# A hybrid streaming layer on one core: the input turned by VectorE, the first weights split as one piece, squares and parameters taken at other places

## The chip, the cores and the metric

One Trainium2 core runs one launch of the kernel. The metric is the device time in microseconds (us), the median over runs. Engines: PE (TensorE) multiplies, PEld is its weight load, DVE is VectorE, ACT is ScalarE, POOL is GpSimd, SP is SyncE, which here only issues DMAs.

## The reference

One layer of a streaming trunk, for 256 prompt tokens and 32 sample tokens (288 columns in all), model width 2048, in fp32:

```python
xn = rmsnorm(x, p['norm_mix_pre'])
proj = xn @ p['w_in']          # columns u 1024 | z 2048 | xBC 2560 | dt 32
u, z, xbc, dt_raw = proj[..., :o1], proj[..., o1:o2], proj[..., o2:o3], proj[..., o3:]
y_pool, new_pool = pool_mixer(u, hist_pool, pos, ...)         # trailing means, 4 groups
y_ssd, new_sconv, new_h = ssd_mixer(z, xbc, dt_raw, ...)      # conv, silu, exact chunked scan, gated norm
mix = jnp.concatenate([y_pool, y_ssd], axis=-1) @ p['w_out']
x = x + rmsnorm(mix, p['norm_mix_post'])
up = rmsnorm(x, p['norm_ffn_pre']) @ p['w_up']                # 2 x 5632 columns
...
f = (jax.nn.silu(gate) * val) @ p['w_down']
x = x + rmsnorm(f, p['norm_ffn_post'])
```

The new states (pooling rows, convolution rows, scan state, FFN rows) are returned too. The change touches the first lines only: the norm of x and the first columns of `proj`.

## The kernel before

Activations are kept feature-major: a K tile holds 128 features on the partitions and the 288 tokens as columns. Weights are the stationary operand, 128 x 128 at a time. Products of fp32 precision are made of three matmuls of rounded parts (`mm3`, L162 to L165): high weight by high activation, high weight by low activation, low weight by high activation. `split_w` (L134) makes the weight's parts: a ScalarE copy for `whi` (L146) and a VectorE subtraction for `wlo` (L147), 1024 columns at a time. `split_from` (L110) makes the activation's, `xn`: L120 on ScalarE with the norm's gain as scale, L121 on VectorE. `project` (L167) runs a list of column groups over the K tiles, with up to five PSUM accumulators (`acc`); three more banks (`aux`) serve everything else. The root mean square is not applied to `xn`, but to the results, as `rstd`, when they leave the accumulators.

The projections of w_in come in this order: a first group of 544 columns (B and C, 512, and dt, 32), then the convolved channels xs in groups of 256 columns, z and u among them; the scan's pieces of work lie between the later ones. The order on each engine is found by a scheduler that simulates the program; `high_priority` moves work ahead in it, `issue_after` and `keep_in_program_order` tie an instruction to another or to the order of the text. A buffer pool with four `raw` buffers holds weights as they land, so SP's issue of a load waits for the buffer's last reader.

The first group runs in K pieces of 2, 2, 4, 4 and 4 tiles. For each piece SP loads the tokens of x (rows on partitions, L294, L295) and the three pieces of weights (256, 256 and 32 columns). `input_tiles` (L292) turns each K tile by three PE transposes (L299 to L301) into an `aux` bank; ScalarE and VectorE read `xn` from there, and VectorE copies the tile to `xT` (L304). ScalarE's queue stores `xT` to DRAM (L306); it is loaded again much later for the residual. The dt columns are split by `split_narrow` (L151), two parts side by side, so that two matmuls of 64 columns (L185, L186) serve them.

The squares for the norm are three ScalarE instructions of 2048 columns with an accumulated sum (L348, L349), then square root, reciprocal, and PE matmuls that spread the result over the partitions (L355), then a copy to `rstd`. `parameters()` (L309), called ahead of the last K piece, turns rows of small parameters by PE (`columns`, L278) with VectorE copies behind.

The DMAs of SP's and of ScalarE's queue share eight completion semaphores in turn: a load waits until the one eight before it has landed.

Of the kernel before, what the change touches and what calls it, by code (L numbers as in the profile page):

```python
# [8 lines left out]
F32 = mybir.dt.float32  # L9
# [7 lines left out]
P = 128  # L17
TC = {"schedule_with_timeline_sim": True}
D_MODEL = 2048
NP_ = 256  # L20
# [20 lines left out]
Z_RATE = (1, 0, 1, 1, 0, 1, 1, 0)  # L41
TAIL = NT - P


@with_exitstack
def body(
# [78 lines left out]

    ahead = [0]

    def fetch_w(view, kb, nk, c0, nc_):
# [21 lines left out]

    def split_narrow(raw, kb, nk, nc_, after):  # L151

        both = xin.tile([P, nk, 2, nc_], F32R, tag="both", bufs=2, name="both")
        with ExitStack() as order:
            order.enter_context(tc.high_priority(offset=ahead[0]))
            for ins in after:
                order.enter_context(tc.issue_after(ins.ins))
            act.activation(both[:, :, 0, :], raw, AF.Copy)
            dve.tensor_tensor(both[:, :, 1, :], raw, both[:, :, 0, :].bitcast(F32), op=ALU.subtract)
        return [(kb + k, both[:, k, :, :].rearrange("p r c -> p (r c)")) for k in range(nk)]  # L160

    def mm3(out, wh, wl, a, start, stop):  # L162
        pe.matmul(out, wh, a[:, 0, :], start=start, stop=False)  # L163
        pe.matmul(out, wh, a[:, 1, :], start=False, stop=False)  # L164
        pe.matmul(out, wl, a[:, 0, :], start=False, stop=stop)  # L165

    def project(view, groups, acts, ksplit, before=None, done=None, spare=(), hold=(), behind=None):  # L167

# [6 lines left out]
        for i, (kb, n) in enumerate(ksplit):  # L175
# [5 lines left out]
            for raw, (c0, w) in zip(raws, groups):  # L181
                if w < P:
                    for k, both in split_narrow(raw, kb, n, w, after or ()):
                        o = accs[m0][: 2 * w, :]
                        pe.matmul(o, both, acts[k][:, 0, :], start=k == k_first, stop=False)  # L185
                        pe.matmul(o, both, acts[k][:, 1, :], start=False, stop=k == k_last)  # L186
                    continue
                parts = split_w(raw, kb, n, w, ((after or ()) if m0 else ()) + (hold if i else ()))
# [23 lines left out]


    ident = const.tile([P, P], F32, name="ident")
    make_identity(nc, ident)
    ones = const.tile([P, P], F32, name="ones")
    pool.memset(ones, 1.0)
    tri = const.tile([P, P], F32, name="tri")
# [5 lines left out]
    warm = const.tile([P, 1], F32, name="warm")  # L224
    tc.keep_in_program_order(act.activation(warm, eps_t, AF.Copy))
    rec = const.tile([P, 16], F32, name="rec")
# [20 lines left out]

    start = ExitStack()
    xin = start.enter_context(tc.tile_pool(name="xin", bufs=1))

    g0_in = xin.tile([KD, P], F32, name="g0_in")
    act.dma_start(out=g0_in, in_=rows(norm_mix_pre))
    pb_in = xin.tile([108, P], F32, name="pb_in")
# [3 lines left out]
    pool.dma_start(out=pb_in[92:108, :], in_=rows(norm_ffn_post))  # L257
    xt = xin.tile([P, 2, D_MODEL], F32, name="xt")
    xs_ = xin.tile([NS, D_MODEL], F32, name="xs_")
    xpv = x_prompt.rearrange("o (b p) d -> p (o b) d", p=P)  # L260
    pa_in = xin.tile([124, P], F32, name="pa_in")
# [15 lines left out]

    def columns(src, n, name):  # L278
        o = const.tile([P, n], F32, name=name)
        p_ = aux([P, n], "pt")  # L280
        pe.transpose(p_, src, ident[:n, :n])
        dve.tensor_copy(o, p_)
        return o

    g_mix_pre = columns(g0_in, KD, "g0")


    xn = []
    xT = xin.tile([P, KD, NT], F32, name="xT")
    xT_d = dram.tile([P, KD, NT], F32, name="xT_d")  # L290

    def input_tiles(kb, n):  # L292
        c = slice(kb * P, (kb + n) * P)
        sp.dma_start(out=xt[:, :, c], in_=xpv[:, :, c])  # L294
        sp.dma_start(out=xs_[:, c], in_=x_sample[0][:, c])  # L295
        for t in range(kb, kb + n):
            p_ = aux([P, NT], "pt")
            c = slice(t * P, (t + 1) * P)
            pe.transpose(p_[:, 0:P], xt[:, 0, c], ident)  # L299
# [4 lines left out]
            dve.tensor_copy(xT[:, t, :], p_)  # L304
            xn.append(a)
        act.dma_start(out=xT_d[:, kb : kb + n, :], in_=xT[:, kb : kb + n, :])  # L306
        return last

    def parameters():  # L309
        pb = columns(pb_in, 108, "pb")  # L310
        g_mix_post = pb[:, 60:76]
        g_ffn_pre = pb[:, 76:92]
        g_ffn_post = pb[:, 92:108]
        pa = columns(pa_in, 124, "pa")
        pah = const.tile([P, 100], F32, name="pah")
        act.activation(pah, pa[:, 0:100], AF.Copy, scale=0.5)
        p_scale = pa[:, 100:108]
        g_ssd = const.tile([P, NX], F32, name="g_ssd")
        act.activation(g_ssd, pa[:, 108:124], AF.Copy, scale=0.5)
        pc = columns(pc_in, 120, "pc")  # L320
        pf = const.tile([P, 6, NF * 2], F32, name="pf")
        for i in range(0, 6, 3):
            p_ = aux([P, 3, NF * 2], "ptf")
            for j in range(3):
                pe.transpose(p_[:, j, :], pf_in[:, i + j, :], ident[: NF * 2, : NF * 2])
            dve.tensor_copy(pf[:, i : i + 3, :], p_)
        return pb, pah, g_mix_post, g_ffn_pre, g_ffn_post, pa, p_scale, g_ssd, pc, pf

    prm = []

    def first_in(kb, n):
        if kb == 12:
            prm.extend(parameters())
        return input_tiles(kb, n)

    win = w_in.rearrange("o (k p) c -> p (o k) c", p=P)
    O_Z, O_X = D_POOL, D_POOL + D_SSD
    O_B, O_C, O_DT = O_X + D_SSD, O_X + D_SSD + 256, O_X + CONV
    first = project(
        win, [(O_B, 256), (O_C, 256), (O_DT, HEADS)], xn, [(0, 2), (2, 2), (4, 4), (8, 4), (12, 4)], first_in  # L340
    )

    ahead[0] = 200
    ssum = xin.tile([P, 3], F32, name="ssum")
    pool.memset(ssum, 1.0)
    junk = xin.tile([P, D_MODEL], F32, name="junk")
    for b in range(2):
        act.activation(junk, xt[:, b, :], AF.Square, accum_out=ssum[:, b : b + 1])  # L348
    act.activation(junk[:NS, :], xs_, AF.Square, accum_out=ssum[:NS, 2:3])  # L349
    rs = xin.tile([P, 3], F32, name="rs")  # L350
    act.activation(rs, ssum, AF.Sqrt, bias=eps_t, scale=1.0 / D_MODEL)
    dve.reciprocal(rs, rs)
    p_ = aux([P, NT], "prs")
    for b, (o, n) in enumerate(BLK):
        pe.matmul(  # L355
            p_[:, o : o + n], rs[:n, b : b + 1].broadcast_to([n, P]), ident[:n, :n], start=True, stop=True
        )
    rstd = const.tile([P, NT], F32, tag="spread", bufs=3, name="rstd")
    dve.tensor_copy(rstd, p_)

    pb, pah, g_mix_post, g_ffn_pre, g_ffn_post, pa, p_scale, g_ssd, pc, pf = prm
    start.close()
# [45 lines left out]

    xs_ps = [project(win, [(O_X, 256)], xn, K16)]
    xs_in = {}  # L410
# [465 lines left out]
    for grp in ((0, 1), (2,), (3,), (4,), (5,), (6,), (7,)):  # L876
# [9 lines left out]
        if grp[0] == 0:  # L886
            sp.dma_start(out=xT, in_=xT_d)
            state_out(sc_stage.rearrange("p s r t -> p s (r t)"), 60, (rows4(new_sconv_p), rows4(new_sconv_s)), op_)
# [146 lines left out]
    fd = dram.tile([NT, D_MODEL], F32, name="fd")  # L1035
    pin = tc.keep_in_program_order

# [184 lines left out]
```

## Time and profile before

| | us |
|---|---|
| median of 3 runs | 1354.11 (1353.88 to 1354.45) |
| the profiled execution, its own time | 1354.27 |
| its span | 1352.6 |
| PE busy | 1340.1 (99%) |
| VectorE busy | 886.6 (66%) |
| ScalarE busy | 669.5 (50%) |
| GpSimd busy | 233.2 (17%) |

The profile is one execution. A group of instructions is given as line, engine, operation, output and inputs with shapes, count, then busy time and mean duration in ns, then the engine's idle time before them with what ended it. A wait row gives what an engine waited for: total, times, longest. A matmul's duration covers its passage through the array; successive ones overlap, so the pitch (start to start) is what counts.

### The profile page before, as it was taken

The numbers are of one execution on the slowest core, as the hardware profiler recorded it, in microseconds if no ns is written. First come the engines' busy times: TensorE is split into PE (matmuls) and PEld (weight loads), VectorE is DVE, ScalarE is ACT, GpSimd is POOL, SyncE is SP. The second block draws the span as 40 slices with busy tenths as digits, with TensorE's granted clock in tenths as the row PEclk, the third lists the DMA queues.
The fourth block names the chain that finished last, engine by engine and source line by source line (L and its number), as shares of the span: only waits on it lengthen the run. The fifth ranks groups of instructions, "written<-read, shape, count | busy, mean of one in ns | idle before, by whom it ended". The sixth has DMA issues, their size and how long they took to land.

```text
span 1352.6 us, 25723 instructions
## 1 busy us (share of the span) xinstructions
PE 1340.1 (99%) x10199; PEld 1327.7 (98%) x10199; DVE 886.6 (66%) x1519; ACT 669.5 (50%) x1003; POOL 233.2 (17%) x394
## 2 busy tenths in 40 slices
PE   8999999999999999999999999999999999999997
PEld 7999999999999999999999999999999999999997
DVE  6898988779644479977676644335666666664454
ACT  6557767446534455645444433334444444454443
POOL 3132112222223320211121100001111111101110
PEclk9999999999999999999999999999999999999999
DMA  8869985464756546876545545554554554576663
GB/s 269 250 192 280 257 249 167 154 221 151 243 179 201 159 132 191 239 196 182 183 156 163 173 144 169 172 179 156 175 168 156 175 169 156 170 232 181 191 182 94
DMA packets 300135, 252.13 MB, mean 186 GB/s; under 512 B 75728, under 2 KB 293050, under 8 KB 299886
## 3 DMA queue, kind: packets, MB, share of 16 engines
q1 hardware_dynamic: 296942, 243.46, 59.0%
q0 software_dynamic: 2320, 4.65, 1.2%
q10 hardware_dynamic: 752, 2.37, 0.5%
q8 instruction: 80, 1.31, 0.4%
q14 instruction: 41, 0.34, 0.1%
HBM read 236.13 MB, written 14.31 MB: 185 GB/s over the span
## 4 chain that ended last, share of the span: by engine, by line
PE 99%; DVE 0%; DMA 0%; ACT 0%; issue 0%; DVEq 0%
PE acc L163 31%; PE acc L165 31%; PE acc L164 31%; PE pst L852 1%; PE py L562 1%; PE acc L1128 1%; PE acc_x L164 0%; PE acc_x L163 0%; PE acc_x L165 0%; PE py L564 0%; DMA xt<-in_x_prompt 0%; PE pt L299 0%; PE acc L1129 0%; PE pt L301 0%; DVE wlo L147 0%; PE acc L186 0%
## 5 line engine op out<-in xcount | busy, mean ns | idle before, releaser
L147 DVE TENSOR_TENSOR wlo<-raw,whi 128x1024 fp32r<-128x1024 f32 (+1 forms) x416 | 493.3, 1188 | 347.9 <-ACT whi L146 346.6
L146 ACT ACTIVATE whi<-raw 128x1024 fp32r<-128x1024 f32 (+1 forms) x416 | 426.6, 1028 | 498.0 <-PE acc L164 421.0
L163 PE MATMUL acc<-hn,whi 128*128 128x288 f32 x1376 | 404.1, 295 | 0.0
L164 PE MATMUL acc<-hn,whi 128*128 128x288 f32 x1376 | 403.6, 294 | 0.3 <-DVE hn L911 0.3
L165 PE MATMUL acc<-hn,wlo 128*128 128x288 f32 x1376 | 403.1, 294 | 0.0
L164 PEld LDWEIGHTS acc<-hn,whi 128*128 128x128 f32 x1376 | 259.7, 189 | 0.7 <-DVE hn L911 0.7
L165 PEld LDWEIGHTS acc<-hn,wlo 128*128 128x128 f32 x1376 | 259.6, 189 | 0.0
L163 PEld LDWEIGHTS acc<-hn,whi 128*128 128x128 f32 x1376 | 257.2, 187 | 0.1
L163 PE MATMUL acc<-xn,whi 128*128 128x288 f32 x704 | 209.3, 299 | 0.0
L164 PE MATMUL acc<-xn,whi 128*128 128x288 f32 x704 | 208.0, 296 | 0.0
L165 PE MATMUL acc<-xn,wlo 128*128 128x288 f32 x704 | 207.2, 296 | 0.0
L163 PE MATMUL acc<-fa,whi 128*128 128x288 f32 x682 | 201.9, 296 | 0.0
L164 PE MATMUL acc<-fa,whi 128*128 128x288 f32 x682 | 201.9, 296 | 0.0
L165 PE MATMUL acc<-fa,wlo 128*128 128x288 f32 x682 | 201.5, 295 | 0.0
L164 PEld LDWEIGHTS acc<-xn,whi 128*128 128x128 f32 x704 | 133.6, 190 | 0.3
L165 PEld LDWEIGHTS acc<-xn,wlo 128*128 128x128 f32 x704 | 132.9, 189 | 0.3
L163 PEld LDWEIGHTS acc<-xn,whi 128*128 128x128 f32 x704 | 132.4, 189 | 0.5
L164 PEld LDWEIGHTS acc<-fa,whi 128*128 128x128 f32 x682 | 128.6, 188 | 0.0
L163 PEld LDWEIGHTS acc<-fa,whi 128*128 128x128 f32 x682 | 128.1, 188 | 0.0
L165 PEld LDWEIGHTS acc<-fa,wlo 128*128 128x128 f32 x682 | 127.9, 188 | 0.0
L945 POOL COPY fc_stage<-ebuf 128x4 f32<-128x4 f32 x88 | 27.8, 316 | 503.6 <-DVE ebuf L944 460.2
L951 DVE SCALAR_TENSOR_TENSOR fc<-ebuf,pf,fc 128x290 f32<-128x290 f32 x176 | 90.4, 517 | 3.1 <-ACT fc L949 0.5
(341 smaller groups left out, 1660.7 us busy)
## 6 DMA issues: line engine op xcount, KB each, us to landing
raw<-in_w_up SPq DMA_DIRECT2D x80, 1024.0 KB, 5.2
raw<-in_w_in SPq DMA_DIRECT2D x40, 1024.0 KB, 5.7
raw<-in_w_down SPq DMA_DIRECT2D x32, 1024.0 KB, 5.3
raw<-in_w_out SPq DMA_DIRECT2D x24, 1024.0 KB, 5.6
raw<-in_w_down SPq DMA_DIRECT2D x16, 768.0 KB, 5.0
raw<-in_w_up SPq DMA_DIRECT2D x14, 512.0 KB, 4.1
gb<-g_d SPq DMA_DIRECT2D x8, 832.0 KB, 5.4
raw<-in_w_in SPq DMA_DIRECT2D x6, 512.0 KB, 6.0
```

Of the source, the lines that this page charges most:

```text
L146: act.activation(hi, raw[:, k : k + n, :], AF.Copy)
L147: dve.tensor_tensor(lo, raw[:, k : k + n, :], hi.bitcast(F32), op=ALU.subtract)
L163: pe.matmul(out, wh, a[:, 0, :], start=start, stop=False)
L164: pe.matmul(out, wh, a[:, 1, :], start=False, stop=False)
L165: pe.matmul(out, wl, a[:, 0, :], start=False, stop=stop)
L562: ins = pe.matmul(y[c, 0:256], xw[:, 0, f_], m[:, h, 0:256], start=True, stop=False)
L852: ins = pe.matmul(st[:, o, :], x_, btok[:, gi, b, :], start=b != 1, stop=b != 0)
L945: pool.tensor_copy(fc_stage[:, :, :, i], e[:, 256:324].rearrange("p (s c) -> p s c", c=34)[:, :, 0:2])
L951: dve.scalar_tensor_tensor(c, e[:, r_ : r_ + 290], pf[:, r_, i : i + 1], c, op0=ALU.mult, op1=ALU.add)
L1128: pin(pe.matmul(o, hi, f2[k][:, :, c], start=k == 0, stop=end, skip_group_check=True))
```

## The change

- At the start, 17 matmuls on constant data whose result nobody reads (`keep_busy`).
- x is loaded in 16 DMAs of 128 KB for the prompt and 8 small ones for the sample, each onto 32 partitions, on SP's and ScalarE's queues. K tiles are made of strided features: tile j of a block of 512 holds features p x 4 + j. The rows of w_in follow the same order. VectorE turns each tile by one transpose in blocks of 32 x 32, reading every fourth column; PE, the PSUM bank and the copy to `xT` are no longer part of it. `xT` tiles lie in the pool of 20 token buffers. The gain of the norm is loaded in this order, without a transpose.
- The first group runs in nine chunks (1, 1, then 2 tiles each). A chunk's weights are one piece of 544 columns: one ScalarE copy for the high part, one more for the dt columns' high part, one VectorE subtraction. Everything in this stage is tied to the order of the text; `prepare(i + 1)` is written ahead of chunk i's products.
- The squares are nine ScalarE instructions of 512 columns: five at the end of `prepare(7)`, four at the end of `prepare(8)`. The first matmul that sums them stands ahead of chunk 7's products, the second one, that spreads `rstd`, ahead of chunk 8's.
- The parameters `pb`, `pa` and `pc` are turned ahead of chunk 5's products and `pf` ahead of chunk 6's, with ScalarE copies instead of VectorE's. 
- `xT` is stored in 16 DMAs by SP, after the loads of the first xs group. Every load of 1 MB of w_in becomes two of 512 KB.

```diff
+NB = 512
+CHUNKS = ((0, 1), (1, 1), (2, 2), (4, 2), (6, 2), (8, 2), (10, 2), (12, 2), (14, 2))
+BUSY = 17
...
     def fetch_w(view, kb, nk, c0, nc_):
-            sp.dma_start(out=raw, in_=view[:, kb : kb + nk, c0 : c0 + nc_])
+            if len(view.shape) == 4:
+                for k in range(kb, kb + nk, 4):
+                    sp.dma_start(out=raw[:, k - kb : k - kb + 4, :], in_=view[:, k // 4, :, c0 : c0 + nc_])
...
+    xt = xin.tile([P, 9, 4, P], F32, name="xt")
+    xpv = x_prompt.rearrange("o (b t) (c i w) -> i t (o b) c w", t=NS, i=4, w=P)
+    win = w_in.rearrange("o (c p j) w -> p (o c) j w", p=P, j=4)
...
+    def sample_load(queue, c):
+        for i in range(4):
+            pin(queue.dma_start(out=xt[NS * i : NS * (i + 1), 8, c, :], in_=xsv[i, :, c, :]))
+    def input_load(queue, c, i):
+        pin(queue.dma_start(out=xt[NS * i : NS * (i + 1), 0:8, c, :], in_=xpv[i][:, :, c, :]))
...
+    for q, i in ((act, 2), (sp, 0), (act, 3), (sp, 1)):
+        input_load(q, 0, i)
+    sample_load(act, slice(0, 1))
+    for kb, n in CHUNKS[:3]:
+        first_load(kb, n)
+    for q, i in ((act, 2), (sp, 0), (act, 3), (sp, 1)):
+        input_load(q, 1, i)
+    sample_load(sp, slice(1, 4))
+    first_load(*CHUNKS[3])
+    for c in (2, 3):
+        for i in range(4):
+            input_load(sp, c, i)
...
-            pe.transpose(p_[:, 0:P], xt[:, 0, c], ident)
-            pe.transpose(p_[:, P:NP_], xt[:, 1, c], ident)
-            pe.transpose(p_[:, NP_:NT], xs_[:, c], ident[:NS, :NS])
-            a = atile("xn")
-            last = split_from(a, p_, g_mix_pre[:, t : t + 1])
-            dve.tensor_copy(xT[:, t, :], p_)
...
+    def prepare(i):
+        kb, n = CHUNKS[i]
+        raw = raws.pop(0)
+        w = xin.tile([P, n, 2 * NB + 3 * HEADS], F32R, tag="w", bufs=4, name="w")
+        hi, lo = w[:, :, : NB + HEADS], w[:, :, NB + HEADS : 2 * (NB + HEADS)]
+        pin(act.activation(hi, raw, AF.Copy))
+        pin(act.activation(w[:, :, 2 * (NB + HEADS) :], raw[:, :, NB:], AF.Copy))
+        for t in tiles:
+            pin(dve.transpose(
+                xT[t].rearrange("p (b t) -> p b t", t=NS),
+                xt[:, :, t // 4, :].rearrange("p b (f j) -> p b f j", j=4)[:, :, :, t % 4],
+            ))
+            pin(act.activation(xn[t][:, 0, :], xT[t], AF.Copy, scale=g_mix_pre[:, t : t + 1]))
+        pin(dve.tensor_tensor(lo, raw, hi.bitcast(F32), op=ALU.subtract))
+        for t in tiles:
+            pin(dve.scalar_tensor_tensor(
+                xn[t][:, 1, :], xT[t], g_mix_pre[:, t : t + 1], xn[t][:, 0, :].bitcast(F32), ...
+        if i + 4 < len(CHUNKS):
+            first_load(*CHUNKS[i + 4])
+        for b in {7: range(5), 8: range(5, 9)}.get(i, ()):
+            pin(act.activation(junk, xt[:, b].rearrange("p c w -> p (c w)"), AF.Square, accum_out=ssum[:, b : b + 1]))
...
+    for i, (kb, n) in enumerate(CHUNKS):
+        if i + 1 < len(CHUNKS):
+            ahead_w.append(prepare(i + 1))
+        if i == 5:
+            pb = columns(pb_in, 108, "pb", copies)
...
+        if i == 7:
+            p_ = aux([P, 9], "prs")
+            pin(pe.matmul(p_, same, ssum, start=True, stop=True))
+            rs = xin.tile([P, 9], F32, name="rs")
+            last_split[:] = [
+                pin(act.activation(rs, p_, AF.Sqrt, bias=eps_t, scale=1.0 / D_MODEL)),
+                pin(dve.reciprocal(rs, rs)),
+            ]
+            pool.tensor_tensor(spots, ...)
+        if i == 8:
+            p_ = aux([P, NT], "prs")
+            pin(pe.matmul(p_, ones, spots.rearrange("p b t -> p (b t)"), start=True, stop=True))
+            rstd = const.tile([P, NT], F32, tag="spread", bufs=3, name="rstd")
+            pin(act.activation(rstd, p_, AF.Copy, scale=0.25))
+        w = ahead_w.pop(0)
...
...
+    xs_ps = [project(win, [(O_X, 256)], xn, K16, wait=last_split)]
+    for t in range(KD):
+        pin(sp.dma_start(out=xT_d[t // 4, :, t % 4, :], in_=xT[t]))
```

More of the change, by code (lines that the diff above doesn't have):

```diff
@@ L130, in fetch_w @@
         with tc.high_priority(offset=ahead[0]):
-            sp.dma_start(out=raw, in_=view[:, kb : kb + nk, c0 : c0 + nc_])
+            if len(view.shape) == 4:
+                for k in range(kb, kb + nk, 4):
+                    sp.dma_start(out=raw[:, k - kb : k - kb + 4, :], in_=view[:, k // 4, :, c0 : c0 + nc_])
+            else:
+                sp.dma_start(out=raw, in_=view[:, kb : kb + nk, c0 : c0 + nc_])
         return raw
@@ L149, in split_w, with mm3, project @@
         return out
[L151 to L167, printed above, removed]
+    def mm3(out, wh, wl, a, start, stop, then=lambda ins: ins):
+        then(pe.matmul(out, wh, a[:, 0, :], start=start, stop=False))
+        then(pe.matmul(out, wh, a[:, 1, :], start=False, stop=False))
+        then(pe.matmul(out, wl, a[:, 0, :], start=False, stop=stop))
+    def project(view, groups, acts, ksplit, before=None, done=None, spare=(), hold=(), behind=None, wait=()):
         n_all = sum(-(-w // P) for _, w in groups)
@@ L181, in project @@
             for raw, (c0, w) in zip(raws, groups):
[L182 to L188, printed above, removed]
+                parts = split_w(raw, kb, n, w, tuple(wait) + ((after or ()) if m0 else ()) + (hold if i else ()))
                 for q, part in enumerate(parts):
@@ L246, in body @@
         ebuf.append(e)
[L248 to L252, printed above, removed]
     pb_in = xin.tile([108, P], F32, name="pb_in")
@@ L276, in body, with columns @@
     )
-    def columns(src, n, name):
+    def columns(src, n, name, copy=None):
         o = const.tile([P, n], F32, name=name)
         p_ = aux([P, n], "pt")
-        pe.transpose(p_, src, ident[:n, :n])
-        dve.tensor_copy(o, p_)
+        pin(pe.transpose(p_, src, ident[:n, :n]))
+        if copy is None:
+            pin(dve.tensor_copy(o, p_))
+        else:
+            copy.append((o, p_))
         return o
-    g_mix_pre = columns(g0_in, KD, "g0")
     xn = []
-    xT = xin.tile([P, KD, NT], F32, name="xT")
@@ L290, in body @@
[L290 to L299, printed above, removed]
-            pe.transpose(p_[:, P:NP_], xt[:, 1, c], ident)
-            pe.transpose(p_[:, NP_:NT], xs_[:, c], ident[:NS, :NS])
-            a = atile("xn")
-            last = split_from(a, p_, g_mix_pre[:, t : t + 1])
[L304 to L341, printed above, removed]
-    ahead[0] = 200
-    ssum = xin.tile([P, 3], F32, name="ssum")
@@ L345, in body @@
[L345 to L357, printed above, removed]
@@ L358, in body, with keep_busy @@
-    rstd = const.tile([P, NT], F32, tag="spread", bufs=3, name="rstd")
-    dve.tensor_copy(rstd, p_)
-    pb, pah, g_mix_post, g_ffn_pre, g_ffn_post, pa, p_scale, g_ssd, pc, pf = prm
+    xT = []
+    xT_d = dram.tile([4, P, 4, NT], F32, name="xT_d")
+    busy_ps = aux([P, NT], "busy_ps")
+    def keep_busy(n):
+        for _ in range(n):
+            pin(pe.matmul(busy_ps, busy[:, 0:P], busy, start=True, stop=True))
+    keep_busy(BUSY)
+    ssum = xin.tile([P, 9], F32, name="ssum")
+    junk = xin.tile([P, D_MODEL // 4], F32, name="junk")
@@ new lines, in body @@
+    early = ExitStack()
+    early.enter_context(tc.high_priority(offset=2000))
+    first = [acc_ps.tile([P, NT], F32, tag="acc", name="acc") for _ in range(5)]
+    ahead_w = [prepare(0)]
+    for i, (kb, n) in enumerate(CHUNKS):
[3 more added lines that the diff above has]
+            pb = columns(pb_in, 108, "pb", copies)
+            pa = columns(pa_in, 124, "pa", copies)
+            pc = columns(pc_in, 120, "pc", copies)
+        if i == 6:
+            for q in range(0, 6, 3):
+                p_ = aux([P, 3, NF * 2], "ptf")
+                for j in range(3):
+                    pin(pe.transpose(p_[:, j, :], pf_in[:, q + j, :], ident[: NF * 2, : NF * 2]))
+                copies.append((pf[:, q : q + 3, :], p_))
+        for o, p_ in copies:
+            pin(act.activation(o, p_, AF.Copy))
+        copies.clear()
+        if i == 7:
[6 more added lines that the diff above has]
+            ]
+            pool.tensor_tensor(
+                spots, rs.unsqueeze(2).broadcast_to([P, 9, NS]), sel4.unsqueeze(1).broadcast_to([P, 9, NS]), op=ALU.mult
+            )
+        if i == 8:
[4 more added lines that the diff above has]
+        w = ahead_w.pop(0)
+        products = [
+            (r, m, k, x) for m in range(4) for k in range(n) for r, x in ((0, 0), (0, 1), (1, 0))
+        ]
+        if i == 0:
+            products.sort(key=lambda q: (q[0], q[3]))
+        for r, m, k, x in products:
+            pin(pe.matmul(
+                first[m], w[:, k, r * (NB + HEADS) + m * P :][:, :P], xn[kb + k][:, x, :],
+                start=kb + k + r + x == 0, stop=kb + k == KD - 1 and r == 1,
+            ))
+        for k in range(n):
+            for x in range(2):
+                pin(pe.matmul(
+                    first[4][: 2 * HEADS, :], w[:, k, 2 * NB + HEADS :], xn[kb + k][:, x, :],
+                    start=kb + k + x == 0, stop=kb + k == KD - 1 and x == 1,
+                ))
@@ L362, in body @@
+    early.close()
+    ahead[0] = 200
+    g_mix_post = pb[:, 60:76]
+    g_ffn_pre = pb[:, 76:92]
+    g_ffn_post = pb[:, 92:108]
+    pah = const.tile([P, 100], F32, name="pah")
+    act.activation(pah, pa[:, 0:100], AF.Copy, scale=0.5)
+    p_scale = pa[:, 100:108]
+    g_ssd = const.tile([P, NX], F32, name="g_ssd")
+    act.activation(g_ssd, pa[:, 108:124], AF.Copy, scale=0.5)
     start.close()
```

47 lines of the change are left out of this document (38 added, 9 removed).

## The prediction

> **What bounds the kernel now.** First the page's busy times, part one: TensorE is the bound as a whole, so only what moves its work or makes it wait can move the end.
>
> ```profile
> span 1352.6 us, 25723 instructions
> PE 1340.1 (99%) x10199; PEld 1327.7 (98%) x10199; DVE 886.6 (66%) x1519; ACT 669.5 (50%) x1003; POOL 233.2 (17%) x394
> ```
>
> Both kernels issue the same work after the first stage, so I cut the span into stretches of 10 us (columns: PE, PEld, DVE, ACT and POOL busy with counts, clock, DMA share, GB/s).
>
> ```profile
> 0.00:10.00 10.00, 4.76 (x20) 3.84 (x21) 5.59 (x12) 4.50 (x9) 8.40 (x45) 1.00 0.72 213
> 10.00:20.00 10.00, 10.00 (x64) 9.11 (x64) 6.23 (x14) 3.92 (x9) 3.48 (x7) 1.00 1.07 331
> 20.00:30.00 10.00, 10.00 (x71) 9.16 (x71) 6.28 (x13) 8.19 (x13) 0.00 (x0) 1.00 0.92 266
> 50.00:60.00 10.00, 10.00 (x78) 10.00 (x77) 8.54 (x17) 7.13 (x11) 2.75 (x4) 1.00 1.07 318
> ```
>
> From 10 us on PE is always busy, and DMA has no spare share while the first weights come. The waits of the first 60 us say the same of PE and ACT: PE's are over by 7 us, ScalarE waits for weights.
>
> ```profile
> PE pt L299 <- DVE xT L304: 1.5, 1, 1.5
> ACT whi L146 <- DMA raw<-in_w_in: 7.0, 5, 3.9
> ```
>
> The timeline gives the pitch of PE: starts 0.24 us apart until 12.1 us, 0.13 after, though the clock column reads 1.00 throughout.
>
> ```profile
> 11.85 0.44 PE L164 MATMUL acc<-xn,whi 128*128 128x288 f32 x1
> 12.09 0.44 PE L165 MATMUL acc<-xn,wlo 128*128 128x288 f32 x1
> ...
> 12.79 0.30 PE L163 MATMUL acc<-xn,whi 128*128 128x288 f32 x1
> 12.93 0.29 PE L164 MATMUL acc<-xn,whi 128*128 128x288 f32 x1
> ```
>
> The groups by form price the parts that come and go:
>
> ```profile
> L299 PE MATMUL pt<-ident,xt 128*128 128x128 f32 x16 | 5.2, 327 | 1.8 <-DVE xT L304 1.5 <-DMA xt<-in_x_prompt 0.3
> L121 DVE SCALAR_TENSOR_TENSOR xn<-pt,g,xn 128x288 fp32r<-128x288 f32 x16 | 8.2, 513 | 7.7 <-ACT xn L120 7.6
> L206 DVE STREAM_TRANSPOSE blocks<-xs 128x288 f32<-128x288 f32 x16 | 7.5, 470 | 11.0 <-DMA xs_d<-blocks 11.0
> ...
> 25.09 1.92 ACT L348 ACTIVATE junk<-xt 128x2048 f32<-128x2048 f32 x1
> 26.89 0.20 ACT L348 ACTIVATION_READ_ACCUMULATOR junk<-xt 128x1 f32 x1
> ```
>
> The landmark: the first group's last matmul starts near 52.37 us, when 27 of the next project are already done. 27 x 0.131 = 3.5, so that group alone ends at 48.84. The change is worth what it does to this number, plus stalls later.
>
> **The change part by part.**
>
> *Turning the input.* Removed are 48 PE transposes. At fast pitch one tile's three take 0.54 (14.51 to 15.05), 8.6 over 16 tiles, all on the path; 16 copies of 0.447 (the group of L304) leave VectorE. Added are 16 stream transposes on VectorE. The nearest row (128x288) takes 0.47, or 0.39 from start to start; with columns at a stride I bound them by 0.39 and 0.94 (twice the row) and take 0.45, since they have the same size and engine.
>
> *PE without waits.* The 17 dummy matmuls fill the time before the first product. On ScalarE's queue nine loads stand before its table load (1.28); a ninth load there waits for an earlier one's semaphore, so its first split starts near 8.8 and the first product near 9.9. 224 matmuls (unchanged in number) x 0.134 = 30.0, two row-sum matmuls 0.25 + 0.48, and some 0.5 of parameters: 41.1, that is 7.7 before 48.84. This is the ceiling of the gain.
>
> *Loads.* Chunk 4 (tiles 6, 7) stands behind all of x, which now comes in 24 small loads, 16 of them of 128 KB. By then 4.59 MB of x and weights and some 0.45 MB of parameters have moved; the trace of before had moved 2.1 MB by 10 us and 5.4 MB by 20 us, so it lands at L = 18.5 to 20.5; I take 19.8. But eight loads are in flight at a time, 29 come before it, and rows of small loads land in 4.3 (32 KB) to 7.7 us (64 KB) on 32 partitions: three and a half such waves give up to 24 or 25 at their middle (6.0), behind a start of 2 and its own landing. I take the curve because the DMA share was already about 1, and keep 25. From L: a chunk of two tiles costs VectorE 1.2 + 2 x (0.39 + 0.43, transpose and xn from start to start) = 2.85, PE 28 x 0.134 = 3.75; PE ends chunk 4 at L + 6.5 = 26.3, 1.3 later than 9.9 + 112 x 0.134.
>
> The Trainium skill ("DMA: Bandwidth & Descriptors", section Bandwidth, Measured) says to batch to 1 MiB for three quarters of peak, and has 138 GB/s at 64 KB against 341 at 1 MB. By it, an estimate, the 2.36 MB of x alone would take over 10 us and L would be about 25; the trace speaks half against it, with loads of 64 KB to 1 MB mixed at 331 GB/s.
>
> *Squares late.* This is the step that matters. All nine squares must end before the row-sum matmul that stands ahead of chunk 7's products, and they stand in ScalarE's order behind the splits of chunks 7 and 8. One of 512 columns: 1.915 x 512/2048 plus a fixed 0.15, plus the accumulator read, some 0.63 to 0.75; I take 0.75, as successive instructions on one engine show small gaps. The other rows of ScalarE, from start to start: a split of 1024 columns 1.00 (two in 2.00), so 1.0 for 1088, with 0.17 for the narrow copy; xn 0.38 each; parameter copies 0.2 for 120 columns, 0.4 for 264 (VectorE's took 0.28 and 0.42). VectorE's subtraction is 1.224 for 1024. From chunk 4 on, ScalarE starts the three parameter copies at L + 7.35 (PE turns them behind chunk 4, then ScalarE's earlier splits end); copies 0.6, split of chunk 7 1.17, xn 0.76 and the two scaled parameters 0.47, five squares 3.75, two parameter copies 0.8, split of chunk 8 1.17, xn 0.76, four squares 3.0: 12.4 in a row, so the squares end at S = L + 19.7 = 39.5. PE has chunk 6 done at 26.3 + 2 x 3.75 + 0.5 = 34.3: it stalls 5.2. Chunk 8 needs nothing later. The end: 39.5 + 0.25 + 3.75 + 0.48 + 3.75 = 47.6 or so. The square root with its table load (1.28), reciprocal and the spots on POOL (1.12 to 1.41, from its adds) fit in chunk 7's 3.75; without that cover they would cost some 3.
>
> *The pitch after the stall.* PE's start shows 0.24 until 12.1, after little work. A stall of 5.2 us may bring it back. The trace of before has no later stall of more than 1.5 us, so the cost is 0 to 5.1/0.24 = 21 matmuls x 0.106 = 2.3; I take 2.0, because the stall is as long as the idle start. The Trainium skill ("TensorE: Matmul & The Clock Gate", Part 1) says that about 3.4 us idle halves the clock and as much work restores it; by it an estimate is 3.4/0.24 x 0.106 = 1.5, against 0 without; no row of before can show it.
>
> *Costed at nothing.* Parameter transposes before S only shorten PE's stall (without it 0.5 to 1.5). Their five copies, moved to ScalarE, are in its row of 12.4. The 16 stores of xT on SP (16 x 0.4 = 6.4) and 40 more issues lie in SP's waits for buffers, 670 us in all; without them the next weights would be 6 us late. The reload of xT is issued at 288 and used at 495. The next project's accumulators are free at S + 7.6 to 8.2, so 0 to 0.3 of stall.
>
> **Sum:** -7.7 + 1.3 + 5.2 + 2.0 = +0.8 (49.6 against 48.84). On the profiled execution's 1354.27 this is 1355.1; that execution stands 0.16 above the median, so 1354.9.
>
> **The rivals.** A measurement of this kernel tells about 0.2%, 2.7 us, from no change.
>
> *Faster.* Loads land by 18.5, PE's products set chunk 4's end (25.0), squares take 0.63 (1.1 less in all) and the pitch holds: S = 25.0 + 0.85 + 12.4 - 1.1 = 37.1, end 45.2, 3.6 gained: 1350.5. For it: the smooth DMA curve. Against: all three must hold. It decides from S + pitch loss below 38.0.
>
> *Slower by loads.* L near 24.5 moves the whole chain by 4.7: end 54.3, 1359.6. For it: the 7.7 us row, and ScalarE waiting for weights already. Against: other loads fill the 16 DMA engines. It is slower by over 0.2% from L = 21.7.
>
> *Slower by VectorE.* Strided transposes at 0.94 add 1.1 a chunk: 4.0 against PE's 3.75, some 3 over the remaining chunks, 1358. Or the token chain: PE's three decay transposes, now at 111.40 with their input ready at 110.22, come after 407 products of the later projects, at S + 8.1 + 54.5 = S + 62.6. VectorE has 51.0 of listed work from its first evacuation (S + 7.3) to their input; with 2 to 6 of waits this is ready at S + 60.3 to 64.3, a stall of up to 1.7: 1356.6. For it: VectorE is 93 to 95% busy from 60 to 200. The first alone crosses the bound.
>
> **How the numbers follow.** My sum 0.45; faster 0.17; loads 0.21; VectorE 0.17, of which 0.14 beyond the bound. The sum's own range (L 19 to 20.5, pitch loss 0 to 2.3, small S errors) is 1352.2 to 1356.6. Point 1354.9. The range takes in most of both sides: from 1350.8 (just short of the faster case) to 1360.0 (the loads). Faster 0.17, same 0.46 (sum nearly whole, minus tails, and the weak VectorE case), slower 0.37.
>
> **What would show it.** No PE transposes of x; stream transposes at 0.39 to 0.5; chunk 4's weights landing near 19.8; a PE wait of about 5 us released by ScalarE's last square, ending near 39.5; matmuls 0.24 apart for 5 us after it; the 224th product near 49.6; nothing new at the decay transposes. A wait at DMA before chunk 4, a square of 0.5 or of 1.0, or a stall after 60 us would make it wrong.

## The result and the profile after

The changed kernel takes 1361.66 us (1360.69 to 1361.76, 4 runs) against 1354.06 in the same runs: a ratio of 1.0054, interval 1.0037 to 1.0072. It is 7.6 slower, where 0.8 was forecast and the range ended at 1360.0. The profiled execution has 1361.63 around a span of 1359.9.

The page and the stretches of 10 us of the changed kernel (columns as in the prediction):

```profile
span 1359.9 us, 25739 instructions
...
PE 1337.2 (98%) x10165; PEld 1327.4 (98%) x10165; DVE 889.3 (65%) x1510; ACT 673.1 (49%) x1024; POOL 231.7 (17%) x395
...
0.00:10.00 10.00, 4.32 (x17) 4.10 (x17) 2.56 (x7) 1.26 (x1) 8.13 (x44) 0.96 0.86 208
10.00:20.00 10.00, 6.04 (x27) 6.00 (x28) 7.35 (x13) 5.99 (x14) 3.96 (x7) 0.53 1.18 211
20.00:30.00 10.00, 9.74 (x74) 9.50 (x73) 7.49 (x13) 5.17 (x10) 0.00 (x0) 1.00 1.00 276
...
40.00:50.00 10.00, 4.15 (x19) 4.01 (x18) 3.93 (x6) 9.88 (x21) 0.67 (x1) 0.66 1.00 327
50.00:60.00 10.00, 10.00 (x76) 9.89 (x75) 7.95 (x19) 4.86 (x8) 1.52 (x5) 1.00 1.03 320
```

Before, PE was busy from 10 us on and DMA moved 331 GB/s in the second stretch. Now DMA is as busy (1.18) but moves 211, and between 40 and 50 it is ScalarE that is full while PE works 4.15. The clock column falls to 0.53 and 0.66, which it did nowhere in this stage before. The waits of the first 70 us, PE's and ScalarE's:

```profile
PE acc L413 <- ACT xn L356: 8.0, 1, 8.0
PE prs L392 <- ACT junk L366: 5.8, 1, 5.8
...
ACT w L347 <- DMA raw<-in_w_in: 4.0, 1, 4.0
```

The timeline of the two engines around those waits:

```profile
13.96 3.25 PE L413 MATMUL acc<-xn,w 128*128 128x288 f32 x12 [7.98 <-ACT xn L356]
...
25.19 1.11 ACT L347 ACTIVATE w<-raw 128x1088 fp32r<-128x1088 f32 x1 [4.01 <-DMA raw<-in_w_in]
...
39.48 0.69 PE L420 MATMUL acc<-xn,w 128*64 128x288 f32 x4
...
45.69 0.19 ACT L366 ACTIVATION_READ_ACCUMULATOR junk<-xt 128x1 f32 x1
...
46.02 0.57 PE L392 MATMUL prs<-ssum,same 128*128 128x9 f32 x2 [5.85 <-ACT junk L366]
46.44 5.06 PE L413 MATMUL acc<-xn,w 128*128 128x288 f32 x24
...
52.13 3.53 PE L413 MATMUL acc<-xn,w 128*128 128x288 f32 x24
...
56.03 0.29 PE L160 MATMUL acc<-xn,whi 128*128 128x288 f32 x1
```

Chunk 4's weights let ScalarE go on at 25.19, the last square is read out at 45.88, PE stalls 5.85, chunk 7's 24 products take 5.06 where chunk 8's take 3.53, and the next project starts at 56.03. Two numbers serve for every run below: the **end** of the first group (the start of the next project's first matmul; 48.84 before, by the landmark of the prediction) and the **remainder** (the span less the end). Before, the remainder is 1352.6 - 48.84 = 1303.8; here it is 1359.9 - 56.03 = 1303.9. The end is 7.2 later and the span 7.3 longer: the whole loss lies in the first group.

Two groups by form give the sizes that the trace of before could not show:

```profile
L351 DVE STREAM_TRANSPOSE xT<-xt 128x288 f32<-128x288 f32 x16 | 10.3, 678 | 8.8 <-DMA xt<-in_x_prompt 8.8
L366 ACT ACTIVATE junk<-xt 128x512 f32<-128x512 f32 x9 | 5.7, 628 | 0.2
```

### The profile page after: what moved, and what is told of

The parts are those of the page before. It is cut to its first block, busy times and chain, and to the rows that moved or that the text cites. A ratio compares the mean times of both kernels' runs of the same rounds, so it can differ in the third digit from the quotient of the medians.

```text
span 1359.9 us, 25739 instructions
## 1 busy us (share of the span) xinstructions
PE 1337.2 (98%) x10165; PEld 1327.4 (98%) x10165; DVE 889.3 (65%) x1510; ACT 673.1 (49%) x1024; POOL 231.7 (17%) x395
## 4 chain that ended last, share of the span: by engine, by line
PE 96%; DMA 1%; DVE 1%; ACT 1%; issue 0%; DVEq 0%; ACTq 0%
PE acc L160 30%; PE acc L162 30%; PE acc L161 30%; DMA raw<-in_w_in 1%; PE pst L927 1%; PE py L637 1%; PE acc L413 1%; PE acc L1202 1%; ACT junk L366 0%; DVE xT L351 0%; PE acc_x L161 0%; DMA xt<-in_x_sample 0%; PE acc_x L160 0%; PE py L639 0%; PE acc_x L162 0%
## 5 line engine op out<-in xcount | busy, mean ns | idle before, releaser
L155 DVE TENSOR_TENSOR wlo<-raw,whi 128x1024 fp32r<-128x1024 f32 (+1 forms) x406 | 483.0, 1191 | 353.1 <-ACT whi L154 351.8
L154 ACT ACTIVATE whi<-raw 128x1024 fp32r<-128x1024 f32 (+1 forms) x406 | 418.4, 1032 | 497.3 <-PE acc L161 423.2
L160 PE MATMUL acc<-xn,whi 128*128 128x288 f32 x640 | 190.3, 297 | 0.0
L161 PE MATMUL acc<-xn,whi 128*128 128x288 f32 x640 | 188.3, 294 | 0.0
L162 PE MATMUL acc<-xn,wlo 128*128 128x288 f32 x640 | 188.1, 294 | 0.0
L162 PEld LDWEIGHTS acc<-xn,wlo 128*128 128x128 f32 x640 | 120.6, 189 | 0.5 <-issue 0.4
L161 PEld LDWEIGHTS acc<-xn,whi 128*128 128x128 f32 x640 | 120.9, 189 | 0.1
L160 PEld LDWEIGHTS acc<-xn,whi 128*128 128x128 f32 x640 | 120.0, 187 | 0.4
```

What stands on the lines that cost most here:

```text
L154: act.activation(hi, raw[:, k : k + n, :], AF.Copy)
L155: dve.tensor_tensor(lo, raw[:, k : k + n, :], hi.bitcast(F32), op=ALU.subtract)
L160: then(pe.matmul(out, wh, a[:, 0, :], start=start, stop=False))
L161: then(pe.matmul(out, wh, a[:, 1, :], start=False, stop=False))
L162: then(pe.matmul(out, wl, a[:, 0, :], start=False, stop=stop))
```

## The experiments

All runs are edits of the changed kernel. The theory was the prediction's own chain, theory C: loads, then ScalarE's row of work up to the last square, then the stall and the pitch; the first rival, P, was PE's own late start.

One thing has to be known to read them. The scheduler lays out the work from some 50 to 210 us anew when an edit moves its simulated times. By the instruction lists, PE's order is that of the changed kernel in e1, e2, e5, e8, e9, e10 and e13, but for at most four matmuls at the very end (VectorE's too, but for at most 17 of its 1510 instructions), and made anew in e3, e4, e6, e7, e11, e12 and e14.

| run | median us | end | remainder |
|---|---|---|---|
| before | 1354.1 | 48.84 | 1303.8 |
| changed | 1361.7 | 56.03 | 1303.9 |
| e1 loads split | 1363.8 | 57.29 | 1303.7 |
| e2 x behind | 1360.2 | 54.57 | 1303.8 |
| e5 all partitions | 1358.6 | 54.23 | 1303.9 |
| e8 longer start | 1362.0 | 56.36 | 1303.6 |
| e9 loads again | 1359.9 | 53.68 | 1303.9 |
| e10 squares spread | 1358.8 | 53.61 | 1303.9 |
| e13 squares spread, all partitions | 1354.2 | 49.02 | 1303.8 |
| new order: e3 stall filled | 1361.9 | 52.43 | 1304.8 |
| e4 wide rows | 1362.5 | 57.31 | 1303.5 |
| e6 sums later | 1364.0 | 54.60 | 1307.0 |
| e7 five squares | 1361.7 | 49.84 | 1311.7 |
| e11 two splits | 1360.5 | 52.67 | 1305.4 |
| e12 five, two splits | 1358.9 | 48.86 | 1308.3 |
| e14 copies back | 1364.0 | 54.46 | 1308.3 |

(Ends and remainders are of the one profiled execution of each, which lies up to 2.9 from its median, most of all in e3. The landing of the loads spreads too: in the seven traces whose loads are the changed kernel's, chunk 4's split starts between 23.46 and 25.30, at 25.19 in the changed kernel itself.)

**Why the weights land late.** Number of loads (e1), order (e2), length of rows (e4), partitions (e5):

```diff
 # e1
-            input_load(sp, c, i)
+            for b in (0, 4):
+                pin(sp.dma_start(out=xt[NS * i : NS * (i + 1), b : b + 4, c, :], in_=xpv[i][:, b : b + 4, c, :]))
```

> The eight loads of x for its last two blocks (128 KB each, behind chunk 3's weights on SP's queue) are cut in two, so 16 loads of 64 KB, with the same bytes in the same 512-byte rows. Theory W (waves: eight loads in flight at a time, so the number of loads sets when chunk 4's weights land): one more wave of 6 to 7.5 us, L from 25.2 to about 32, time about 1361.7 + 6 = 1368. Theory B (bytes: rows of 512 bytes onto 32 partitions move at some 200 GB/s, and the bytes ahead set L): L within 1 us of 25.2, time 1361 to 1362.5.

Chunk 4's split starts at 25.57 instead of 25.19, after the same wait of 4.0: eight loads more cost 0.4, not a wave of six, though these weights were issued 3.9 later (at 21.52 instead of 17.60). The loads of 64 KB land in 3.4, those of 128 KB in 7.4. Theory W falls, and with it the reason that the prediction gave for late loads. The time is 2.1 up, 1.3 of it in the end, mostly because chunk 7 ran at the slow pitch for longer (6.07 instead of 5.06); the rest is spread between executions.

```diff
 # e2: c = 2, 3 no longer loaded ahead of the chunks
         first_load(*CHUNKS[i + 4])
+        for q in range(4) if i < 2 else ():
+            input_load(sp, 2 + i, q)
```

> The loads of the third block of x are issued behind chunk 4's weights, those of the fourth behind chunk 5's; nothing else moves. Theory C (ScalarE's row of work from chunk 4's weights on sets the end of the first group): chunk 4's weights are issued when their buffer is free, near 14.0 instead of 17.6, and land 3 to 4 us sooner; the last square, the first row-sum matmul and the end move with them: 1358.0 to 1359.0. Rival P (TensorE's own late and slow start sets the end, the squares only fill): no change, 1361 to 1362.

Chunk 4's wait is gone (its split starts at 21.20), but the next two chunks now wait 1.8 each, the end is 1.5 earlier and the time 1.5 shorter: half of what was expected. The order of the loads moves the wait; the time for their bytes stays.

```diff
 # e4
-    win = w_in.rearrange("o (c p j) w -> p (o c) j w", p=P, j=4)
+    win = w_in.rearrange("o (c p j) w -> p (o c) j w", p=P, j=8)
 ...                # x, gain, xT alike: two blocks of 1024 features
```

> K tiles of every eighth feature instead of every fourth, so x comes in rows of 1 KB: 8 loads of 256 KB and 8 of the sample, the rows of the first input weights permuted to match; all of the first half of x must land before the first transpose. Theory B (bytes in short rows): the rate in 10 to 20 us rises from 211 GB/s toward the 331 of before, L to 20 to 22, time 1357 to 1358.5. Theory W (number of loads): seven loads fewer ahead, almost a wave, L also some 5 sooner, so this run with the split loads tells: both together favour W, this one alone B. If transposes of every eighth column are slower than 0.61 us, VectorE takes back what they lose.

No gain. While x comes, from 12 to 18 us, the rate is 193 to 221 GB/s, no better with rows of 1 KB. The weights are no longer waited for, but the first product is at 16.96, since half of x must be there, and from there VectorE paces the chunks (3.3 each). The rate speaks against short rows as the whole cause. It does not clear them: by the transfer records of the first 30 us, a row of 1 KB kept its DMA engine for 75 ns on average and one of 512 bytes for 45, so per byte the longer row is cheaper by a sixth.

```diff
 # e5
-        pin(queue.dma_start(out=xt[NS * i : NS * (i + 1), 0:8, c, :], in_=xpv[i][:, :, c, :]))
+        pin(queue.dma_start(out=xt[:, 2 * i : 2 * i + 2, c, :],
+                            in_=xrow[:, :, 512 * c + P * i : 512 * c + P * (i + 1)]))
```

> The 16 loads of the prompt keep their number, size (128 KB), place in the queues and 512-byte rows, but each lands on all 128 partitions (two tokens' rows each) instead of 32. This leaves out the arrangement that the transposes need: what they turn is not x's tiles, so the numbers of the output are not the layer's; the work and the waits stay. Theory N (loads onto 32 partitions are slow for the DMA engines): the rate in 16 to 22 us rises from some 200 to 300 GB/s, chunk 4's weights land by 22 to 23 instead of 25.2, the end 2 to 4 sooner: 1358 to 1359.5. Theory R (512-byte rows, or the issue times, set it): no change, 1361 to 1362.5.

Same number, size and row length of loads, 128 partitions: 3.1 faster, as theory N said. The stretch of 16 to 22 us, first of the changed kernel, then of this run:

```profile
16.00:22.00 6.00, 6.00 (x36) 5.96 (x35) 6.00 (x10) 4.08 (x8) 0.00 (x0) 0.72 1.19 199
```

```profile
16.00:22.00 6.00, 6.00 (x37) 5.97 (x37) 6.00 (x10) 3.56 (x8) 0.00 (x0) 0.76 1.13 308
```

About the same DMA share moves 308 GB/s instead of 199, and chunk 4's split starts at 22.37. Not all of the step from 199 to 308 is the partitions. The transfers of the same stretches, again the changed kernel's first (the counts add up from left to right):

```profile
DMA packets 2025, 1.20 MB, mean 199 GB/s; under 512 B 167, under 2 KB 1923, under 8 KB 2025
```

```profile
DMA packets 2177, 1.85 MB, mean 308 GB/s; under 512 B 161, under 2 KB 1716, under 8 KB 2177
```

The changed kernel moves 1756 rows of 512 bytes, which are x's, and 102 longer ones; e5 moves 1555 and 461, because the last row of x starts at 20.2 and the weights' rows of 2176 bytes follow. By the transfer records, a row of 512 bytes kept its engine for 50 ns there and for 37 here, so the partitions are worth a factor of 1.4. Over the first 30 us it is 44.8 against 32.4 ns, on 4680 rows and 16 engines 3.6 us. Loads onto a quarter of the partitions keep the DMA engines busy for longer per byte. The short rows remain dearer even here: 15.8 bytes per ns, where the weights' rows have 20.5. The Trainium skill ("DMA: Bandwidth & Descriptors", section Rules for kernel authors) asks for 128 partitions and 1 MiB per DMA for full bandwidth; the first half is what this run shows, and no run here tests the second.

**Whether PE's start counts.**

```diff
-BUSY = 17
+BUSY = 60
```

> 60 instead of 17 matmuls on constant data at the start, so TensorE is busy until about 12 and the clock should still be full when the first product comes at 14.0; its first 28 products take 3.8 instead of 6.2 us. Theory C: TensorE is not on the path before chunk 7, so no gain, 1361.2 to 1361.9. Rival P (TensorE's late and slow start is the bound): 2 to 2.5 gained, 1359.3.

The first 28 products take 4.1 instead of 6.2, and PE then waits for chunks 2 and 4 instead: 1362.0, no gain. Rival P falls. It also shows why 17 constant matmuls did not help: they were over at 6, eight us before the first product, and the first 21 products of the changed kernel are 0.24 apart.

**What the stall does to the pitch.**

```diff
         if i == 7:
+            fill_ps = aux([P, NT], "fill_ps")
+            for _ in range(40):
+                pin(pe.matmul(fill_ps, busy[:, 0:P], busy, start=True, stop=True))
```

> 40 matmuls on constant data, read by nobody, stand ahead of the first row-sum matmul, in the place where TensorE waits for the last square (5.85 us). If the idle time is what made the next 24 matmuls 0.2 us apart instead of 0.134, the fill keeps the pitch: -1.5 to -1.7, about 1360.0, and the granted clock of that stretch reads 1.00. If the pitch comes from chunk 7's own operands, no gain: 1361.7, or up to 0.5 more.

```profile
38.31 5.43 PE L393 MATMUL fill_ps<-busy 128*128 128x288 f32 x40
...
44.46 3.42 PE L416 MATMUL acc<-xn,w 128*128 128x288 f32 x24
```

Chunk 7's 24 products take 3.42 instead of 5.06 behind a stall of 0.5, and the clock reads 1.00, so the idle time costs 1.6. In this execution the loads also came 1.7 sooner by themselves. The median did not move (1361.85), over runs from 1358.96 to 1364.23; what spread them so far was not found, so the gain is shown in the trace alone.

**The squares.** One chunk more before their sum (e6), four left out (e7), and e7 with fewer splits ahead of rstd (e12):

```diff
 # e6
-        if i == 7:
+        if i == 8:
             p_ = aux([P, 9], "prs")
 ...                # the second sum and rstd: behind the loop
 # e7
-        for b in {7: range(5), 8: range(5, 9)}.get(i, ()):
+        for b in {7: range(5), 8: ()}.get(i, ()):
 # e12, on e7
-    xs_ps = [project(win, [(O_X, 256)], xn, K16, wait=last_split)]
+    xs_ps = [project(win, [(O_X, 256)], xn, K16, wait=last_split, hold=(rstd_ins,))]
```

> The first row-sum matmul stands one chunk later, ahead of chunk 8's products, and the second, with the copy to rstd, behind them; the squares stay where they are. Theory C (TensorE's 5.85 us at this matmul is what chunk 7 loses): chunk 7 runs at 40.2 to 44.0 without a stall, the wait for the last square is about 2 ahead of chunk 8, and the accumulators come free 1 to 1.5 late behind rstd: 3.5 to 4.5 gained, 1357.2 to 1358.2. Rival: the whole gain is given back at the accumulators, whose evacuation waits for rstd behind ScalarE's four splits: 1360.5 to 1361.7.

> The four squares of chunk 8's preparation are left out (the sums of four blocks of tokens keep a constant, so their scale is wrong). Theory C (ScalarE's row of work from chunk 4's weights to the last square sets the end): the sums wait only for the fifth square, 40.4, TensorE is there at 40.2, so no stall and no lost pitch; chunk 8 has its parts near 42 to 44: 7 to 7.6 gained, 1354.0 to 1354.7, unless a later chain stands behind it (the token chain's slack was 1.2). Rival P (TensorE's start is the bound): under 3 gained.

> The run with five squares (four left out, so the scale of four blocks is wrong), with only two of the four splits ahead of rstd. There the first group ended at 49.0, but 1311.7 came after it instead of 1303.8, with a lead of 0.7. Theory V: the first group ends at 49 again, the lead is over 2, what comes after falls to 1304 to 1306, time 1355 to 1357. Rival (the order of the later work, made anew by the scheduler, costs it, whatever the lead): 1360 to 1363.

In e7 the stall at the sums is gone, and the first group's last product starts near 49, seven sooner, as theory C had it. In e6 the stall is 2.2, but PE then waits 2.3 for the accumulators, and the end is only 1.4 sooner. Yet neither is faster in time: the remainder grew by 3.1 and 7.8. In e7, PE's waits over the whole span include:

```profile
PE acc L162 <- DVE wlo L155: 4.8, 3, 2.9
...
PE py L638 <- DVE m L626: 1.2, 1, 1.2
...
PE acc L160 <- DVE ebuf L455: 0.7, 1, 0.7
```

The three waits for `wlo` end at 166, 203 and 213 us: VectorE's splits of later weights come late. I took this for a lead that VectorE had lost (theory V: its first evacuation 2.59 ahead of the end in the changed kernel, 0.67 in e7). e12 has a lead of 2.07 and a remainder 3.3 smaller, not the 6 to 8 that V wanted.

**Loads and squares together.** e9 reorders all loads (the sample's first part early, seven instead of nine on ScalarE's queue, x's last blocks behind chunks 4 and 5); e10 also spreads the squares and makes BUSY 36; e11 is e10 with the `hold` of e12; e13 is e10 with the loads of e5.

```diff
 # e10, on e9
-        for b in {7: range(5), 8: range(5, 9)}.get(i, ()):
+        for b in {5: range(2), 6: range(2, 4), 7: range(4, 6), 8: range(6, 9)}.get(i, ()):
```

> Same computation and same order of all work on TensorE and VectorE as in the changed kernel; only loads are issued otherwise: the sample's first part right behind x's first block, all of x's second block on SP's queue, so that ScalarE's queue holds seven loads instead of nine, x's third block behind chunk 4's weights and the fourth behind chunk 5's. Theory C (the end of the first group follows ScalarE's row of work, which starts with the loads): first product 10.5 to 12 instead of 14.0, no wait at chunk 4's weights over 1.0, last square 41 to 43 instead of 45.9, end of the first group 51.5 to 53, what comes after it unchanged at 1303.8, time 1357 to 1358.7. If an earlier end is given back later even in the same order: 1360 to 1362.

> The loads of the run before, 36 constant matmuls at the start, and the nine squares spread over the preparations of chunks 5 to 8 (2, 2, 2, 3), where ScalarE waits for VectorE's transposes. TensorE's order stays that of the changed kernel. Theory C: last square 37 to 39.5, end of the first group 45.5 to 48.5. Theory V (VectorE must begin the evacuation some 2.6 before TensorE starts the next project, or TensorE waits for it later, because VectorE is nearly full until 200 us): rstd comes some 7.4 behind the last square, the lead shrinks to 1 or less, and 1 to 5 of the gain are given back after 60 us: 1352 to 1357. Without theory V the time is 1351 to 1354.

> As the run before, and of the four splits of the next project's weights that ScalarE and VectorE do ahead of rstd only two stay ahead of it. Theory V: the evacuation starts some 2 earlier, the lead is 2 to 3 again, and what is given back after 60 us falls under 1: 1 to 3 faster than the run before. If the gain is lost to the scheduler's new order instead, no better than the run before, within 1.

> The run with the squares spread and the loads reordered, with x's 16 loads landing on all 128 partitions as in the run that did this alone (the arrangement for the transposes is left out, so the output is not the layer's). TensorE's order is that of the changed kernel. If loads onto 32 partitions and the squares in ScalarE's row together are the whole loss: no wait of ScalarE for weights over 1, last square 39 to 40.5, end of the first group 47.5 to 50, as early as before's 48.84, and with 1303.8 to 1304.8 behind it 1353 to 1356. If something else in the stage holds it: the end of the first group stays over 51.5, time over 1357.

e9's first product is at 11.24, but ScalarE still waits 6.6 for weights, the worst for chunk 5, and the end of 53.7 and the time miss what was expected. e10 waits 4.4, 3.6 of it in one piece until 26.68, and from there its row to the last square is full: 1358.8 and an end of 53.6, not 45.5 to 48.5. That row takes 16.4 us, where e9's from the same split takes 18.5: the spread squares shorten it by 2, but the split starts 1.3 later in this trace, and PE still waits 4.3 for the last square. e11 is not faster than e10; its lead is 2.59, as in the changed kernel, and yet PE waits 1.7 for `wlo` near 197. With that theory V is refused as the whole reason.

e13 differs from e10 by the destination of x's loads alone. Chunk 5's split, first in e10, then in e13:

```profile
26.68 1.11 ACT L346 ACTIVATE w<-raw 128x1088 fp32r<-128x1088 f32 x1 [3.64 <-DMA raw<-in_w_in]
```

```profile
21.71 1.12 ACT L347 ACTIVATE w<-raw 128x1088 fp32r<-128x1088 f32 x1 [0.63 <-DMA raw<-in_w_in]
```

It starts 5.0 sooner, the end is 4.6 sooner and the time 4.5 shorter (1354.2 for 1358.8). PE's waits and timeline in e13:

```profile
PE prs L394 <- ACT junk L368: 3.0, 1, 3.0
PE acc L415 <- ACT xn L356: 1.7, 1, 1.7
```

```profile
38.54 5.95 PE L415 MATMUL acc<-xn,w 128*128 128x288 f32 x24
...
49.02 0.29 PE L160 MATMUL acc<-xn,whi 128*128 128x288 f32 x1
```

The last square ends at 37.98 (sooner than expected), chunk 7 still loses its pitch behind a stall of 3.0, and the end is 49.02 (48.84 before), the remainder 1303.8, the time 1354.24: a ratio to before of 1.0003 (0.9993 to 1.0012). So the loss is undone in two steps: 2.9 from the changed kernel to e10 (the order of the loads, the spread squares, and 36 constant matmuls, not separated here) and 4.5 by the partitions alone. No run has the partitions and the order of the loads without the spread squares, so what these add by themselves stays open. And an end seven us earlier is not given back as such: in the changed kernel's own order the remainder stays at 1303.6 to 1303.9 for ends from 49.0 to 57.3. So the early end by itself did not eat the gain in e7; its new order, its short lead or both did.

**The parameter copies.**

```diff
-            pin(act.activation(o, p_, AF.Copy))
+            pin(dve.tensor_copy(o, p_))
```

> The five copies of turned parameters go back from ScalarE to VectorE; all else as in the changed kernel. ScalarE's row from chunk 4's weights to the last square loses 1.2 (measured 0.46 + 0.65 with their gaps), VectorE's gains 1.4 in a stage where it has 2.7 idle before chunk 8. Theory C: last square 44.7 to 45.2, end of the first group 1 earlier, time 1360.3 to 1361. If VectorE paces the stage instead: unchanged or up to 1 later.

From chunk 4's split (24.08) to the last square (44.66) it is 20.6, against 20.7: the copies on ScalarE cost 0.1, because VectorE paces the chunks meanwhile. The time is 2.4 longer, through a new order that has PE wait 2.9 for `wlo` near 200, with a lead of 2.59 once more.

No version here that computes the layer beats the kernel before; e10 is 4.8 behind.

## Why the prediction was wrong

- *Loads: the step that failed.* The prediction put chunk 4's weights at 19.8, on the curve of bytes moved before, "because the DMA share was already about 1". They were there at 25.19, 5.4 later (3.7 to 5.5 over the seven traces with these loads). The share was near 1 again, but in 16 to 22 us it stood for 199 GB/s, where before it had stood for 309 in the same stretch: what failed is the step from a full share to the old rate. Onto all 128 partitions, in the same order, the weights were there at 22.37 (e5), so the partitions are 2.8 of the 5.4 here (1.1 to 2.9 against the seven traces), and 5.0 at chunk 5 from e10 to e13. Why e5 is still 2.6 later than 19.8 stays open; x's shorter rows would fit, but no run has longer rows on all partitions. The rival "slower by loads" had the size (24.5, 1359.6) and got 0.21; its reason, eight loads in flight, was wrong (e1). The estimate of about 25 from the size of the loads came out too, but partly by luck: e5 keeps the size, and its weights are there at 22.37.
- *Turning the input.* 0.61 from start to start was inside the bounds (0.39 to 0.94) but over the 0.45 taken: a chunk costs VectorE 3.2, not 2.85. This is most of the 1.0 by which S came later behind L (20.7 for 19.7).
- *Squares late.* 0.76 from start to start against 0.75, and the stall 5.85 against 5.2. The mechanism stood as described.
- *The pitch.* 1.7 against 2.0: 5.43 for chunk 7's 28 products instead of 3.75. What this saved went to small gaps: from S to the end it is 10.15, where 8.1 + 2.0 was reckoned.
- *The first product* came at 14.0 instead of 9.9, because VectorE's first transpose waited for x until 12.65. It had no effect on the end: PE still reached the sums 5.85 before the last square, and a full pitch at the start gained nothing (e8).
- *Costed at nothing.* Right in sum: the remainder moved by 0.1. The token chain had no stall in the changed order. (VectorE, there said to be 93 to 95% busy from 60 to 200 us, is only 87% busy from 100 to 140 in the trace of before (34.7 of 40), so this rival had more room than it was given.)

The sum with the measured terms: 49.6 + 5.4 + 1.0 = 56.0, against 56.03. So one term moved the forecast from "the same" to "slower" by the prediction's own bound of 0.2%, and the range's end (1360.0) was 1.7 short because the case of late loads was computed with L at 24.5 and S at L + 19.7: L came 0.7 later than that and S a further 1.0.

## What to carry to other kernels

A DMA share near 1 says that the engines are busy, not what they move: price a new load by the rate of rows with the same shape of destination, and where there is none, let the worse bound carry more weight. When a kernel's order comes from a scheduler's simulation, split each time into the end of the edited stage and the remainder; only runs with the same instruction order tell what an earlier end is worth. An engine's row of work that starts with a load, here ScalarE's 20 us, moved as one piece with that load (e5: both 2.8 sooner), and spreading its parts gained only where that engine had waited (2 us in e10).

## What was not expected

- Loads of 128 KB with rows of 512 bytes kept a DMA engine for 44.8 ns a row onto 32 partitions and 32.4 onto 128. Rows of 1 KB onto 32 partitions were cheaper per byte by a sixth only, and brought no gain in time.
- Stream transposes of 128x288 take 0.68 when they read every fourth column, against 0.47 before with contiguous ones.
- The granted clock shows in some profiles only: 0.53 in 10 to 20 us and 0.66 in 40 to 50 here, with the slow pitch of 0.24. The slow start of before, at the same pitch, had read 1.00, and so do e2, e3, e4 and e14 in 10 to 20 us, where the products begin 0.24 apart as well. The pitch is the safer sign. The Trainium skill ("TensorE: Matmul & The Clock Gate", Part 1) has half clock after some 3.4 us idle; stalls of 8.0 and 5.85 agree, and those of 3.0 in e13 and 2.2 in e6 were followed by 5.95 and 4.96 for 24 products, so here shorter ones cost pitch too (one of 0.85 in e7 did not: 3.54).
- The order that the scheduler made anew moved the remainder by -0.4 to +7.8 in seven edits, none of which was aimed at the work behind 60 us. Why VectorE's splits come late in five of them was not settled: a short lead explains part of e7 at most.
